# Forming the masked BK·AR products of both heads in one visit of TensorE, alternating row halves and PSUM banks, in a streaming encoder layer

## The chip, the cores and the metric

The kernel runs on one core of a Trainium2 chip. The metric is the device time of one execution in microseconds. The time before is the median of three runs.

## The reference

One layer of a hybrid encoder: differential attention and an RWKV-7 recurrence side by side, fed by one projection and closed by one output projection. Cut to what the change touches:

```
proj = rms_norm(x) @ w_in                        # 1024 prompt + 32 sample tokens, 2048 -> 8320 columns
q, k, v, g_att, p_rw, g_rw = split(proj)
att = diff_attention(q, k, v) * silu(g_att)      # 8 heads, two maps each
r, k, v, w, a = ...                              # token shift and LoRAs of p_rw; 16 heads of 64
for t in tokens:                                 # per head, S is 64 x 64
    sa = S @ a_t
    S = S * w_t + sa b_t^T + v_t k_t^T
    y_t = S @ r_t
out = x + concat(att, norm(y) * silu(g_rw)) @ w_out
```

The kernel works through the recurrence in chunks of 64 tokens. For each chunk and head it needs the products of the scaled keys with the scaled queries inside the chunk: `BK` (64 channels x two sets of 64 tokens) against `AR` (the same shape), 128 x 128 numbers, masked to the causal triangle.

## The kernel before, in words

**Tiling.** The tokens are worked in two halves: half A with 544 columns (512 prompt, 32 sample; 9 chunks) and half B with 512 (8 chunks). A unit `u` (0 to 15) is one half and one of 8 head pairs: one attention head and two RWKV heads, whose 64 channels lie in partitions 0 to 63 (`low`) and 64 to 127 (`high`). Per unit the main loop runs eight projections (`proj`, line 353), each a run of matmuls of 128 columns of weights against 256, 288 or 512 tokens into a PSUM tile `pj`; every weight is split into a rounded part and a remainder (`wh`, `wl`), every input likewise (`xh`, `xl`), so that three matmuls stand for one product. After the units come 16 output projections for each half.

**Who goes between.** Everything else is written as generators in six streams (`chs`, `dns`, `qks`, `pos`, `ats`, `los`). Between groups of projection matmuls `pump` (line 156) lets each stream take a step that is due. A step yields the nanoseconds after which the next may follow, and, if it names one, the PSUM bank that it wants. `clk` is the planner's own count of TensorE time, to which `mm` (line 83) adds what it takes a matmul to cost; `ready` says when it takes a bank to be free (900 ns after use for `am`, 2208 for `Y`, from the table `LAT`). This fixes the order of the program when it is built; on the chip the engines keep that order and wait on semaphores. PSUM has one buffer of `am` (attention, the block sums `blkr` of q and k, the post-processing) and one of `Y` (all that `rw_down` and `rw_decay` form).

**The step of the change.** `rw_down` (line 718) prepares a sub-block of a head pair: four or five chunks. The chunks are taken four at a time, so a sub-block of five has a second group of one chunk. For each group and each of the two heads there is one visit: wait for `Y`, form `BK` times `AR` for each chunk into its 128 columns of the bank (line 762, booked under line 92), and let VectorE multiply by the mask into `MM` (line 765). The matmuls are full fp32, which shows as two records each in the trace; they use 64 rows of the array, the lower ones for head 0, the upper for head 1. Behind them `MM` goes out by DMA, a forward substitution on VectorE (lines 784 and 786) solves it, and `rw_chain` goes on.

Of the kernel before, what the change touches and what calls it, by code (L numbers as in the profile page):

```python
# [12 lines left out]
F32R = mybir.dt.float32r  # L13
# [33 lines left out]
def build(tc, I, O):  # L47
# [16 lines left out]
    clk = [0.0]  # L64
    ready = {"am": 0.0, "Y": 0.0}

    def am():
        ready["am"] = None
        return PT("am", 1)

    def ym():
        ready["Y"] = None
        return PT("Y", 1)
# [6 lines left out]
            clk[0] += 95.0  # L80
            mode[0] = now

    def mm(out, lhsT, rhs, start=True, stop=True):
        n, m = 1, 1
        for d in rhs.shape[1:]:
            n *= d
        for d in lhsT.shape[1:]:
            m *= d
        shaped(lhsT.shape[0], m)
        load = 0.83 * m + 5.0  # L90
        clk[0] += max(0.4375 * n + 6.0, load) if rhs.dtype == F32R else 2 * max(0.84 * n, load)
        PE.matmul(out, lhsT, rhs, start=start, stop=stop)  # L92

    def tr(out, in_, idn):
# [9 lines left out]
    class Stream:  # L104
# [11 lines left out]
        def due(self):  # L116
            if self.cur is None and not self.q or self.cond is not None and not self.cond():
                return None
            return max(self.at, ready[self.am]) if self.am else self.at

        def run(self):
            c = clk[0]
# [3 lines left out]
        def step(self):  # L126
            if self.cur is None:
                if not self.q:
                    return False
                self.cur = self.q.pop(0)  # L130
            if self.cond is not None and not self.cond():
                return False
            if self.due() > clk[0]:
                return False
            self.cond, self.am = None, None
            try:
                y = next(self.cur[1])
            except StopIteration:
                self.done.add(self.cur[0])
                self.cur = None  # L140
                y = 0
            for r in ready:
                if ready[r] is None:
                    ready[r] = clk[0] + LAT[r]
            if callable(y):
                self.cond = y
            elif isinstance(y, tuple):
                self.at, self.am = clk[0] + y[0], y[1]
            else:
                self.at = clk[0] + y  # L150
            return True
# [106 lines left out]
    for k, tag in enumerate(RAW):  # L258
# [7 lines left out]
        a, eng = (acc[1], G) if pool else (acc[0], V)  # L266
# [131 lines left out]
    low, high = slice(0, 64), slice(64, 128)  # L398
# [9 lines left out]
    def lat(key, half):  # L408
        return LAT[key + "AB"[half]]
# [308 lines left out]
    def rw_down(half, i, sub, st):  # L718
# [8 lines left out]
        c_, a = st["ca"][:, 0, lo:hi], st["ca"][:, 1, lo:hi]  # L727
        P3 = st["P3"][:, lo:hi]
        r, k, v = st["rk"][:, 0, lo:hi], st["rk"][:, 1, lo:hi], st["v"][:, lo:hi]
        BK = T([128, cn, 2, 64], "BK")  # L730
# [22 lines left out]
        key = "ms"  # L753
        for c0 in range(0, cn, 4):
            m = min(4, cn - c0)
            for h in range(2):
                yield lat(key, half), "Y"
                key = "ms2"
                hr = (low, high)[h]
                p = ym()  # L760
                for j in range(m):
                    mm(p[:, 128 * j:128 * j + 128],
                       BK[hr, c0 + j].rearrange("p a t -> p (a t)"),
                       AR[hr, c0 + j].rearrange("p a t -> p (a t)"))
                V.tensor_tensor(MM[:, c0:c0 + m, h, :].rearrange("p c (x t) -> p c x t", t=64)[:, :, 0:3:2, :],  # L765
                                p[:, :128 * m].rearrange("p (a x t) -> p a x t", x=2, t=64),
                                mask.rearrange("p (x t) -> p x t", x=2).unsqueeze(1).to_broadcast([128, m, 2, 64]),
                                op=ALU.mult)
        MMg = MM.rearrange("p c h t -> p (c h) t")
# [390 lines left out]
```

## Time and the profile before

| | |
|---|---|
| time, median of 3 runs | 2612.89 us (2607.87 to 2619.28) |
| the profiled execution | 2613.46 us; span 2611.7 us from its first to its last instruction |
| TensorE matmul busy | 2549.7 us, 98% |
| TensorE weight load busy | 2220.1 us, 85% |
| VectorE busy | 1892.0 us, 72% |
| ScalarE, GpSimd busy | 1349.6 us (52%), 415.1 us (16%) |
| granted TensorE clock, mean | 0.995 of full speed |

Busy times are shares of the whole span. A matmul's record is longer than the time that it takes from its neighbours, since records overlap; what one costs is read from the starts.

### The profile page before, as it was taken

To read this page: it belongs to the slowest core of one execution; us is meant where nothing else is said; L and a number is where in the kernel's file an instruction comes from. 1 tells how busy PE (TensorE), PEld (TensorE's weight loads), DVE (VectorE), ACT (ScalarE), POOL (GpSimd) and SP (SyncE) were. 2 spreads that over 40 slices of the span, in tenths; PEclk is the share of its full clock that TensorE was granted. 3 is DMA by queue.
4 is the path that set the end of the run, shared out by engine and by line. 5 is a ranking of instruction groups with operands and counts; after the bars stand their busy time and mean duration, and the time that the engine had idled before them with its cause. 6 is when DMAs were issued, how large, how long until landed. Compare 5 with 4: busy or idle time off the path is not lost. (4 is left out here: it accounts for less than half of the span.)

```text
span 2611.7 us, 49090 instructions
## 1 busy us (share of the span) xinstructions
PE 2549.7 (98%) x17128; PEld 2220.1 (85%) x17128; DVE 1892.0 (72%) x5768; ACT 1349.6 (52%) x3138; POOL 415.1 (16%) x949
## 2 busy tenths in 40 slices
PE   7999999999999999999999999999999999999999
PEld 7999999999898999877777777777777778999887
DVE  7576877777777787788787887788878888753432
ACT  6455555555555655565555555555555556332321
POOL 3211111111111111111111111111111111111000
PEclk9999999999999999999999999999999999999999
DMA  4433332324242524353332323232324244544443
GB/s 156 119 102 94 93 103 84 110 82 115 75 122 80 170 72 122 98 153 100 98 98 87 103 83 106 85 111 81 114 81 115 77 132 118 176 148 140 137 142 108
DMA packets 198665, 286.74 MB, mean 110 GB/s; under 512 B 102097, under 2 KB 115921, under 8 KB 198417
## 3 DMA queue, kind: packets, MB, share of 16 engines
q0 software_dynamic: 51088, 169.12, 21.8%
q1 hardware_dynamic: 147328, 114.47, 15.5%
q8 instruction: 136, 2.23, 0.4%
q14 instruction: 113, 0.92, 0.1%
HBM read 228.11 MB, written 37.51 MB: 102 GB/s over the span
## 5 line engine op out<-in xcount | busy, mean ns | idle before, releaser
L92 PE MATMUL pj<-xh,wh 128*128 128x256 f32 (+2 forms) x3888 | 1294.2, 333 | 7.7 <-ACT xh L248 6.7
L92 PE MATMUL pj<-xl,wh 128*128 128x256 f32 (+2 forms) x3888 | 1274.7, 328 | 5.0 <-DVE xl L249 5.0
L92 PE MATMUL pj<-xh,wl 128*128 128x256 f32 (+2 forms) x3888 | 1272.5, 327 | 1.1 <-DVE wl L225 1.1
L92 PEld LDWEIGHTS pj<-xh,wh 128*128 128x128 f32 x3888 | 735.7, 189 | 61.2 <-ACT xh L248 7.0
L92 PEld LDWEIGHTS pj<-xl,wh 128*128 128x128 f32 x3888 | 736.2, 189 | 52.5 <-DVE xl L249 8.8
L92 PEld LDWEIGHTS pj<-xh,wl 128*128 128x128 f32 x3888 | 735.4, 189 | 52.4 <-DVE wl L225 2.1
L224 ACT CAST wh<-wr 128x512 fp32r<-128x512 f32 x584 | 360.6, 618 | 471.8 <-PE pj L92 420.1
L225 DVE TENSOR_TENSOR wl<-wr,wh 128x512 fp32r<-128x512 f32 x584 | 401.2, 688 | 193.5 <-ACT wh L224 162.9
L231 POOL DMA_DIRECT2D wr<-w_in x517 | 278.3, 538 | 1639.8 <-DVE wl L225 492.2
L786 DVE TENSOR_TENSOR ts<-tm,ts 64x54 f32<-64x54 f32 (+35 forms) x992 | 198.2, 200 | 15.1
L784 DVE TENSOR_TENSOR tm<-ts,ms 64x54 f32<-64x54 f32 (+35 forms) x992 | 197.7, 199 | 14.5 <-DMA ts<-tinit 0.2
L92 PEld LDWEIGHTS ch<-UV,MM 64*64 64x64 f32 (+2 forms) x1632 | 111.5, 145 | 38.1 <-DVE UV L903 9.2
L92 PE MATMUL ch<-UV,MM 64*64 64x64 f32 (+2 forms) x1632 | 128.9, 231 | 8.0 <-DVE UV L846 5.1
L899 ACT ACTIVATE SP<-Sw,PL 64x64 f32<-64x64 f32 x256 | 88.3, 345 | 91.2 <-DVE Sw L908 78.1
L225 DVE TENSOR_TENSOR wl<-MM,wh 128x512 fp32r<-128x512 f32 x64 | 44.0, 689 | 89.1 <-ACT wh L224 89.1
L224 ACT CAST wh<-MM 128x512 fp32r<-128x512 f32 x64 | 39.6, 620 | 128.9 <-PE pj L92 123.3
L896 DVE TENSOR_TENSOR xs<-ch,MM 64x64 f32<-64x64 f32 x272 | 58.6, 216 | 50.2 <-ACT RS L893 45.7
L908 DVE SCALAR_TENSOR_TENSOR Sw<-ch,PL,SP 64x64 f32<-64x64 f32 x256 | 70.7, 276 | 23.2 <-PE ch L92 16.7
L92 PE MATMUL am<-Vt,E 128*128 128x128 f32 (+1 forms) x592 | 84.7, 280 | 1.8 <-ACT wh L224 1.1
L92 PE MATMUL Y<-AR,BK 64*128 64x128 f32 x544 | 84.8, 290 | 0.7 <-DVE MM L765 0.6
L92 PEld LDWEIGHTS Y<-AR,BK 64*128 64x128 f32 x544 | 67.5, 188 | 19.8 <-issue 9.1
L92 PEld LDWEIGHTS am<-Vt,E 128*128 128x128 f32 (+1 forms) x592 | 73.5, 189 | 8.7 <-issue 2.6
(303 smaller groups left out, 3127.9 us busy)
## 6 DMA issues: line engine op xcount, KB each, us to landing
wr<-w_in POOLq DMA_DIRECT2D x517, 256.0 KB, 3.2
wr<-w_out POOLq DMA_DIRECT2D x64, 256.0 KB, 3.6
MM<-w_out POOLq DMA_DIRECT2D x32, 512.0 KB, 4.0
t<-xB SPq DMA_DIRECT2D x32, 256.0 KB
ms<-dm SPq DMA_DIRECT2D x96, 64.0 KB
t<-t SPq DMA_DIRECT2D x64, 68.0 KB
t<-mixd SPq DMA_DIRECT2D x16, 272.0 KB
t<-xA SPq DMA_DIRECT2D x16, 272.0 KB
```

Of the source, the lines that this page charges most:

```text
L92: PE.matmul(out, lhsT, rhs, start=start, stop=stop)
L224: S.copy(wh, raw)
L225: V.tensor_tensor(wl, raw, wh.bitcast(F32), op=ALU.subtract)
L231: q.dma_start(raw, wsrc[:, g * 512:(g + 1) * 512].rearrange("p (k f) -> p k f", k=4))
L784: V.tensor_tensor(tm, ts_[:, 0:qn, s:s + 1].to_broadcast([R * nb, qn, m]), ms[:, s:s + 1, s + 1:32].to_broadcast([R * nb, qn, m]), op=ALU. ...
L786: V.tensor_tensor(ts_[:, 0:qn, s + 1:32], tm, ts_[:, 0:qn, s + 1:32], op=ALU.add)
L896: V.tensor_tensor(xs[64 * h:64 * h + 64], ch[low, 64 * h:64 * h + 64], MM[low, c, h, 0:64], op=ALU.add)
L899: S.activation(SP[:, h, :], S_[hr, h, :], AF.Copy, scale=PL[hr, 0, gc:gc + 1])
L908: V.scalar_tensor_tensor(S_[hr, h, :], ch[low, 192 + 64 * h:256 + 64 * h], PL[low, h, gc:gc + 1], SP[:, h, :], ALU.mult, ALU.add)
```

## The change

The two visits of the two heads become one. It asks for both banks, `Y` for head 0 and `am` for head 1, and issues the chunks' matmuls in turn, low rows into `Y`, high rows into `am`. The two VectorE multiplications follow. The planner learns three things: a matmul may be booked at half its cost (`ways=2`), a step may name several banks, and it is due when the last of them is ready. The number of matmuls (272, 544 records), of VectorE multiplications (80) and of DMAs is as before.

```diff
-    def mm(out, lhsT, rhs, start=True, stop=True):
+    def mm(out, lhsT, rhs, start=True, stop=True, ways=1):
...
-        clk[0] += max(0.4375 * n + 6.0, load) if rhs.dtype == F32R else 2 * max(0.84 * n, load)
+        clk[0] += (max(0.4375 * n + 6.0, load) if rhs.dtype == F32R else 2 * max(0.84 * n, load)) / ways
...
-            return max(self.at, ready[self.am]) if self.am else self.at
+            return max(self.at, *(ready[a] for a in self.am)) if self.am else self.at
...
-                self.at, self.am = clk[0] + y[0], y[1]
+                self.at, self.am = clk[0] + y[0], y[1:]
...
         for c0 in range(0, cn, 4):
             m = min(4, cn - c0)
+            yield lat(key, half), "Y", "am"
+            key = "ms2"
+            ps2 = (ym(), am())
+            for j in range(m):
+                for h, hr in enumerate((low, high)):
+                    mm(ps2[h][:, 128 * j:128 * j + 128],
+                       BK[hr, c0 + j].rearrange("p a t -> p (a t)"),
+                       AR[hr, c0 + j].rearrange("p a t -> p (a t)"), ways=2)
             for h in range(2):
-                yield lat(key, half), "Y"
-                key = "ms2"
-                hr = (low, high)[h]
-                p = ym()
-                for j in range(m):
-                    mm(p[:, 128 * j:128 * j + 128],
-                       BK[hr, c0 + j].rearrange("p a t -> p (a t)"),
-                       AR[hr, c0 + j].rearrange("p a t -> p (a t)"))
                 V.tensor_tensor(MM[:, c0:c0 + m, h, :].rearrange("p c (x t) -> p c x t", t=64)[:, :, 0:3:2, :],
-                                p[:, :128 * m].rearrange("p (a x t) -> p a x t", x=2, t=64),
+                                ps2[h][:, :128 * m].rearrange("p (a x t) -> p a x t", x=2, t=64),
```

Since `clk` moves less, the whole order behind the first such visit is another one. Three places show it.

On TensorE, the first visit of the program, as a difference (`Y_` and `am_` are the two PSUM banks, `sc_` the attention's transposes):

```order
-L92 MATMUL Y_1720<-AR_1615,BK_1551 128x128 x4
-L97 MATMUL sc_1727<-cst_250,E_294_1627 128x128 x4
+L92 MATMUL Y_1720<-AR_1615,BK_1551 128x128
+L92 MATMUL am_1721<-AR_1615,BK_1551 128x128
+L92 MATMUL Y_1720<-AR_1615,BK_1551 128x128
+L92 MATMUL am_1721<-AR_1615,BK_1551 128x128
+L92 MATMUL Y_1720<-AR_1615,BK_1551 128x128
+L92 MATMUL am_1721<-AR_1615,BK_1551 128x128
+L92 MATMUL Y_1720<-AR_1615,BK_1551 128x128
+L92 MATMUL am_1721<-AR_1615,BK_1551 128x128
+L97 MATMUL sc_1841<-cst_250,E_294_1627 128x128 x4
```

Four matmuls of one head became eight that alternate; the second visit, which stood 27 rows further on, is gone.

On TensorE again, the visit of unit 10's second sub-block (half B), which runs among the projections of unit 11. Before, where the block sum of q, `am_22528<-p,blkr`, stands three and two rows above the first that is shown:

```order
L92 MATMUL pj_22497<-xl_2894_15717,wh_22518 128x512
L92 MATMUL pj_22497<-xh_2893_15716,wl_22519 128x512
L92 MATMUL pj_22497<-xh_2896_15722,wh_22518 128x512
L92 MATMUL pj_22497<-xl_2897_15723,wh_22518 128x512
L92 MATMUL pj_22497<-xh_2896_15722,wl_22519 128x512
L92 MATMUL pj_22497<-xh_2917_15828,wh_22552 128x512
L92 MATMUL pj_22497<-xl_2918_15829,wh_22552 128x512
L92 MATMUL pj_22497<-xh_2917_15828,wl_22553 128x512
L92 MATMUL pj_22497<-xh_2920_15834,wh_22552 128x512
L92 MATMUL pj_22497<-xl_2921_15835,wh_22552 128x512
L92 MATMUL pj_22497<-xh_2920_15834,wl_22553 128x512
L92 MATMUL Y_22562<-AR_22464,BK_22419 128x128 x4
```

And of the change, from the last matmul of the visit on:

```order
L92 MATMUL am_22529<-AR_22446,BK_22403 128x128
L92 MATMUL pj_22497<-xh_2897_15729,wh_22518 128x512
L92 MATMUL pj_22497<-xl_2898_15730,wh_22518 128x512
L92 MATMUL pj_22497<-xh_2897_15729,wl_22519 128x512
L92 MATMUL pj_22497<-xh_2900_15735,wh_22518 128x512
L92 MATMUL pj_22497<-xl_2901_15736,wh_22518 128x512
L92 MATMUL pj_22497<-xh_2900_15735,wl_22519 128x512
L92 MATMUL pj_22497<-xh_2948_15932,wh_22672 128x512
L92 MATMUL am_22654<-p_4398_22487,blkr_252 128x512
L92 MATMUL am_22654<-p_4399_22488,blkr_252 128x512
```

The visit now stands ahead of the block sum, and seven projection matmuls lie between the last use of `am` and the next. The same seven stand there for units 8, 10, 12 and 14. In half A there are seven places with 12 or 13 projection matmuls of 256 to 288 tokens between a visit and a block sum in `am`: five behind the one-chunk group and two (units 1 and 4) behind the group of four.

On VectorE at the same place, the change's rows up to the second mask multiplication:

```order
L786 TENSOR_TENSOR ts_22157<-tm_22186,ts_22157 64x3x22
L784 TENSOR_TENSOR tm_22189<-ts_22157,ms_22152 64x63
L786 TENSOR_TENSOR ts_22157<-tm_22189,ts_22157 64x3x21
L225 TENSOR_TENSOR wl_22704<-wr_22701,wh_22703 128x512
L784 TENSOR_TENSOR tm_22192<-ts_22157,ms_22152 64x60
L402 TENSOR_TENSOR p_4399_22488<-t_22484,p_4398_22487 128x512
L786 TENSOR_TENSOR ts_22157<-tm_22192,ts_22157 64x3x20
L402 TENSOR_TENSOR kk_22692<-bo_22689,p_4450_22691 128x256
L784 TENSOR_TENSOR tm_22195<-ts_22157,ms_22152 64x76
L765 TENSOR_TENSOR MM_22454<-Y_22528,cst_250 128x4x2x64
L786 TENSOR_TENSOR ts_22157<-tm_22195,ts_22157 64x4x19
L765 TENSOR_TENSOR MM_22454<-am_22529,cst_250 128x4x2x64
```

The write of `BK` by line 750, for which the visit waits, stands six rows above the first one shown (between them lie rows of lines 784, 351, 786, 803 and 784). The multiplication that empties `am` is the 17th row behind it.

## Rows read from the trace of the kernel before

**Rows 1.** The page's parts 1 and 2: busy time, share of the span and instructions of each engine; the granted clock in 40 slices, in tenths.

```profile
span 2611.7 us, 49090 instructions
PE 2549.7 (98%) x17128; PEld 2220.1 (85%) x17128; DVE 1892.0 (72%) x5768; ACT 1349.6 (52%) x3138; POOL 415.1 (16%) x949
PEclk9999999999999999999999999999999999999999
```

**Rows 2.** The end of the chain that ended last, in order of time: start, us, what.

```profile
2342.09 265.94 PE pj L92 x1476
2608.05 0.69 DVE t L968
```

**Rows 3.** The groups of the step, shapes kept apart: line, engine, operation, count | busy us, mean ns | idle before.

```profile
L92 PE MATMUL Y<-AR,BK 64*128 64x128 f32 x544 | 84.8, 290 | 0.7 <-DVE MM L765 0.6
L765 DVE TENSOR_TENSOR MM<-Y,cst 128x512 f32<-128x512 f32 x64 | 43.7, 682 | 4.4 <-PE Y L92 3.9
L765 DVE TENSOR_TENSOR MM<-Y,cst 128x128 f32<-128x128 f32 x16 | 4.6, 285 | 1.5 <-PE Y L92 1.1
```

**Rows 4.** The timeline around a visit of four chunks (eight records), TensorE and then the VectorE row that empties the bank: start us, us, engine, line, tiles.

```profile
146.68 0.29 PE L92 MATMUL pj<-xl,wh 128*128 128x288 f32 x1
146.81 0.29 PE L92 MATMUL pj<-xh,wl 128*128 128x288 f32 x1
147.04 1.16 PE L92 MATMUL Y<-AR,BK 64*128 64x128 f32 x8
148.12 0.40 PE L92 MATMUL pj<-xh,wh 128*128 128x288 f32 x1
...
148.24 0.68 DVE L765 TENSOR_TENSOR MM<-Y,cst 128x512 f32<-128x512 f32 x1
```

**Rows 5.** The same around a visit of one chunk (two records), and the VectorE row that empties the bank.

```profile
179.76 0.29 PE L92 MATMUL pj<-xh,wl 128*128 128x288 f32 x1
179.99 0.48 PE L92 MATMUL Y<-AR,BK 64*128 64x128 f32 x2
180.40 0.40 PE L92 MATMUL pj<-xh,wh 128*128 128x288 f32 x1
...
182.51 0.28 DVE L765 TENSOR_TENSOR MM<-Y,cst 128x128 f32<-128x128 f32 x1
```

**Rows 6.** The timeline of TensorE around two visits of line 863: matmuls of 64 rows and 64 columns whose outputs alternate between partitions 0 to 63 and 64 to 127; 16 records, and 20.

```profile
210.67 0.29 PE L92 MATMUL pj<-xl,wh 128*128 128x288 f32 x1
210.90 0.68 PE L92 MATMUL ch<-UV,MM 64*64 64x64 f32 x16
211.51 0.40 PE L92 MATMUL pj<-xh,wl 128*128 128x288 f32 x1
...
255.86 0.29 PE L92 MATMUL pj<-xh,wl 128*128 128x288 f32 x1
256.09 0.80 PE L92 MATMUL ch<-UV,MM 64*64 64x64 f32 x20
256.81 0.40 PE L92 MATMUL pj<-xh,wh 128*128 128x288 f32 x1
```

**Rows 7.** The timeline of TensorE at line 906: weights of 128 columns, 64 moving columns, four records.

```profile
223.47 0.63 PE L92 MATMUL ch<-UV,MM 128*128 128x64 f32 x4
223.91 0.36 PE L92 MATMUL pj<-xh,wl 128*128 128x256 f32 x1
```

**Rows 8.** The timeline at a visit of four chunks in half A (second sub-block), TensorE and the VectorE row that empties its bank.

```profile
310.26 1.16 PE L92 MATMUL Y<-AR,BK 64*128 64x128 f32 x8
...
312.33 0.68 DVE L765 TENSOR_TENSOR MM<-Y,cst 128x512 f32<-128x512 f32 x1
```

**Rows 9.** The timeline at the two visits of unit 10's second sub-block (half B), TensorE and VectorE in order of time. In brackets is the idle time before a row, and what ended it.

```profile
1569.02 0.41 DVE L750 TENSOR_TENSOR BK<-rk,ca 128x256 f32<-128x256 f32 x1
1569.35 0.22 DVE L786 TENSOR_TENSOR ts<-tm,ts 64x72 f32<-64x72 f32 x1
1569.50 0.34 DVE L514 SCALAR_TENSOR_TENSOR asg<-am,cvec,asg 128x128 f32<-128x128 f32 x1
1569.90 0.68 DVE L402 TENSOR_TENSOR p<-t,p 128x512 fp32r<-128x512 f32 x1
...
1569.98 0.47 PE L92 MATMUL am<-p,blkr 128*128 128x512 f32 x1 [0.91 <-DVE tm L784]
1571.22 0.39 PE L92 MATMUL pj<-xh,wh 128*128 128x512 f32 x1
1571.45 0.39 PE L92 MATMUL pj<-xl,wh 128*128 128x512 f32 x1
...
1571.46 0.47 DVE L803 SCALAR_TENSOR_TENSOR bo<-rk,par 128x256 f32<-128x256 f32 x1
1572.00 1.16 PE L92 MATMUL Y<-AR,BK 64*128 64x128 f32 x8
1578.25 0.68 DVE L765 TENSOR_TENSOR MM<-Y,cst 128x512 f32<-128x512 f32 x1
1579.07 1.13 PE L92 MATMUL Y<-AR,BK 64*128 64x128 f32 x8 [0.40 <-DVE MM L765]
```

**Rows 10.** Groups of VectorE that stand in the queue there: line, operation, count | busy us, mean ns of one | idle before.

```profile
L225 DVE TENSOR_TENSOR wl<-wr,wh 128x512 fp32r<-128x512 f32 x584 | 401.2, 688 | 193.5 <-ACT wh L224 162.9 <-PE pj L92 20.4 <-PE Y L92 3.2
L351 DVE TENSOR_TENSOR t<-pj,rb 128x512 f32<-128x512 f32 x24 | 16.3, 680 | 0.8 <-PE pj L92 0.6
L402 DVE TENSOR_TENSOR kk<-bo,p 128x256 fp32r<-128x256 f32 x24 | 10.0, 416 | 0.5 <-ACT p L401 0.5
L786 DVE TENSOR_TENSOR ts<-tm,ts 64x60 f32<-64x60 f32 x72 | 15.0, 209 | 1.2
```

## The prediction

> **What bounds the kernel now.** I read the page first. TensorE is busy for 98% of the span at a full granted clock; no other engine passes 72%, weight loads apart [rows 1]. The chain that ended last closes with 266 us of projection matmuls without a wait and one VectorE addition [rows 2]. So a microsecond less on TensorE is a microsecond less in the end, as long as no new wait takes its place, and one less on VectorE is worth nothing by itself. Next I read the groups of the step: 544 records of `Y<-AR,BK`, and 64 + 16 mask multiplications, which tells that there are 64 visits of four chunks and 16 of one [rows 3]. What a visit costs is in the timeline, from the starts of its neighbours: two projection matmuls start 0.13 us apart; with a visit of eight records between them it is 1.31 us (146.81 to 148.12), so the visit takes 1.18 [rows 4]. The visit of two records takes 0.64 - 0.13 = 0.51 [rows 5]. Six records more cost 0.67, so a record costs 0.112, and 0.51 - 2 x 0.112 = 0.29 us is a fixed price for going to 64 rows and coming back. In all the step holds TensorE for 64 x 1.18 + 16 x 0.51 = 83.7 us.
>
> **What goes, part one: the fixed price.** Eighty visits become forty: 32 of sixteen records and 8 of four. That saves 40 x 0.29 = 11.6 us however the records run, since alternation stays within one shape (64 rows, 128 columns).
>
> **Part two: whether the two row halves overlap.** The trace of before has no visit that alternates rows. Its nearest rows alternate columns, at line 863. Sixteen records take 0.84 - 0.13 = 0.71 us there, twenty take 0.82 [rows 6]: 0.11 for four more, 0.029 each (the starts carry two decimals). Alone, a record of 64 columns should take half of what 128 take, 0.056. So alternation between two parts of the array runs nearly two at a time, weight loads included, at 0.52 of the price. By that a record of the new visit costs 0.0585, a visit of sixteen 0.29 + 16 x 0.0585 = 1.23 in place of 2.36, one of four 0.52 in place of 1.02. The sum is 32 x 1.13 + 8 x 0.50 = 40.2 us, fixed price included. The other end is no overlap at all: records go on at 0.112 and 11.6 us stay. What speaks for that end is line 906: weights of 128 columns against only 64 moving columns take 0.44 us for four records [rows 7], again 0.11, so loading 128 columns is by itself as dear as a record, and if two row halves share one way for their weights nothing can overlap. The column rows show two loads of 64 columns side by side, not two of 128. I take 40.2, as that row is the only one in which two parts of the array alternate.
>
> The Trainium skill, "TensorE: Matmul & The Clock Gate", section "Part 3: Packing small matmuls — row/col tiling", has matmuls of separate row tiles run concurrently and gives 3.07x for four of them, not the full four. As an estimate from that page, two tiles at the same efficiency would be 1.53x, a record 0.073, the saving 32 us. No run here shows it yet, and the sum does not use it.
>
> **Part three: what is added, the wait for `am`.** VectorE does the same 80 multiplications. But head 1's product now sits in `am`, which the block sums and the attention want back, and VectorE empties it second. What counts is how late VectorE comes and how soon TensorE wants the bank.
> - Behind a visit of one chunk VectorE came 2.04 us after the last record's end (180.47 to 182.51) in one place [rows 5] and 0.04 us after a visit of four in another (148.20 to 148.24) [rows 4]. In the changed order five one-chunk visits are followed by a block sum after 12 or 13 projection matmuls, which is 1.5 us behind that end. Two multiplications of 0.285 [rows 3] after 2.04 free the bank at 2.6: a stall of 1.1. After 0.04 there is none. I take half, 5 x 0.55 = 2.8 (0 to 5.6).
> - At two places in half A a group of four is followed as soon. VectorE came 0.91 late in such a place (311.42 to 312.33) [rows 8]; with 2 x 0.68 the bank is free at 2.27, 0.8 after it is wanted: 1.6 in all (0 to 1.6).
> - At four places of half B the visit moves ahead of a block sum that used to precede it. Behind the write of `BK` VectorE has 17 rows up to the second multiplication: ten of 0.21, and 0.68, 0.47, 0.69, 0.68, 0.42 and twice 0.68 [rows 3, 9, 10], 6.4 us by durations and some 5.1 with the 0.075 by which neighbours overlap (1569.43 against 1569.35) [rows 9]. TensorE wants `am` after the visit (1.23) and seven matmuls at 0.23 [rows 9], 2.9 us after `BK`: a stall of 2.2. Before, TensorE idled there for 0.91, waiting for `am`, and for 0.40 at the second visit [rows 9]. The first wait stays, as the visit needs `am` and `BK` as well; the second goes. Net 4 x 1.8 = 7.2. If TensorE comes as late as it did (1572.00, 2.6 behind `BK`) nothing stalls and 4 x 1.3 = 5.2 is won; without overlap on VectorE it is 4 x (3.5 - 0.4) = 12.4.
>
> Together 11.6 us, from -5.2 to 19.6. Behind a stalled block sum stand the projection matmuls themselves, so nothing hides it; ScalarE's square roots and the rotary step follow later and are not on the path.
>
> **Priced at nothing.** A second wait of one visit per group falls away, so the forward substitution starts a few microseconds sooner; it is VectorE work under TensorE, and VectorE has 28% to spare [rows 1]. The two multiplications come back to back, which holds a weight split (0.69, line 225) up by at most 0.68 per visit; without its cover by the weights already split that would be 40 x 0.68 = 27 us, but the idle time before matmuls of `Y<-AR,BK` that a late multiplication caused was 0.6 us in the whole span [rows 3]. The rest of the order is the same work at other places.
>
> **The sum.** The profiled execution took 2613.46 us (span 2611.7 and 1.8 around it), 0.6 over the median of 2612.89. 2613.5 - 40.2 + 11.6 = 2584.9, so **2585 us**, 1.1% less.
>
> **The rivals.** A measurement of this kernel can tell about 0.5%, 13 us, from no change.
> - *No overlap.* Loading 128 columns of weights is the limit in both row halves. Then 2613.5 - 11.6 + 11.6 = 2613: the change doesn't do what it says. For it: the 0.11 of line 906 [rows 7]. Against it: the column rows [rows 6], whose loads ran side by side. 13%.
> - *Half an overlap.* A record costs 0.085, midway: a visit of sixteen 1.65, of four 0.63, saving 32 x 0.71 + 8 x 0.39 = 25.8; 2613.5 - 25.8 + 11.6 = 2599 us. It needs a part of each record, its load or its start, that stays serial; the 0.029 for 0.028 of the column rows speaks against one [rows 6]. 12%. (The Trainium skill's 3.07x, cited above, points this way.)
> - *VectorE empties `am` too late (slower).* In 20 or so places the bank is wanted within some 2 us. If VectorE lagged there as it did behind the visit at 1572.00, 5.1 us (1573.16 to 1578.25) [rows 9], each would stall for 5.1 + 1.36 - 1.5 = 5.0: 2613.5 - 40.2 + 20 x 5.0 = 2673. It loses from 40.2 / 20 = 2.0 us a place, by more than 0.5% from 2.7. Against it: in that stretch VectorE had rows ahead that the changed order puts elsewhere, and in half A the lags are 0.04 to 2.04. 7%. The Trainium skill, "TensorEngine Tiling (Array Packing)", section "PSUM Bottleneck", warns of just this: tiling speeds TensorE up and not the emptying of PSUM. The trace agrees in that line 765's time can't shrink [rows 3].
> - *The forecast*, overlap with the waits of part three, 2568 to 2597: 68%.
>
> **Range and chances.** The low end is the overlap with the least waits, 2613.5 - 40.2 - 5.2 = 2568; the high end is no overlap, 2613. Beyond it lie the late `am` and little else. The likeliest case's own range is 2568 to 2597. Faster by over 0.5% (under 2600): 68% and two thirds of the half overlap, 76%. Within: no overlap and the rest of the half, 17%. Slower: 7%.
>
> **What would show it.** In the profile after, the records of a visit of sixteen should span about as long as eight do now, 1.2 us, with starts in pairs; if they span 2.0 there is no overlap and the forecast is wrong by 29 us. TensorE's busy time should fall with the span. Idle time ahead of the block sums `am<-p,blkr` that ends with line 765 prices part three; over 1 us a visit would break the forecast, and a stall at a place of which nothing is said here would, too.

## The result, and the profile after

The changed kernel takes 2600.78 us (median of 20 executions, 2594.68 to 2609.74) against 2614.46 us for the kernel before in the same session: a ratio of 0.9945, 95% interval 0.9933 to 0.9956. That is 14 us less, a little under half of the 28.6 forecast; the median lies inside the range, and the forecast of 2585 was 16 us too low. One execution of the experiment e12 took 5011 us, nearly twice as long as its others, and is left out of every figure below.

The page's heads, answering to [rows 1], and the mean granted clock:

```profile
span 2603.7 us, 49027 instructions
PE 2518.3 (97%) x17128; PEld 2205.2 (85%) x17128; DVE 1897.8 (73%) x5768; ACT 1347.3 (52%) x3138; POOL 418.6 (16%) x949
PEclk9999999999999899999999999999999999999999
```

```profile
core 0: 2603.7 us, clock 0.986
```

TensorE is busy 31 us less, but the span fell by only 8, and one slice of the clock shows an 8 where [rows 1] had none. The mean clock was 0.995 before. The profiled execution took 2605.68 us and is one of the slower of the 20.

**The step itself** came out as forecast. The groups, answering to [rows 3], and the first visit, answering to [rows 4] (start us, us, engine, line, tiles):

```profile
L92 PE MATMUL Y<-AR,BK 64*128 64x128 f32 x272 | 41.6, 288 | 0.0
L92 PE MATMUL am<-AR,BK 64*128 64x128 f32 x272 | 41.4, 288 | 0.4 <-DVE asg L514 0.4
L765 DVE TENSOR_TENSOR MM<-Y,cst 128x512 f32<-128x512 f32 x32 | 21.9, 683 | 0.4
L765 DVE TENSOR_TENSOR MM<-am,cst 128x512 f32<-128x512 f32 x32 | 21.8, 680 | 1.1 <-PE am L92 1.1
```

```profile
140.75 0.28 PE L92 MATMUL pj<-xh,wl 128*128 128x256 f32 x1
140.96 0.37 PE L92 MATMUL Y<-AR,BK 64*128 64x128 f32 x1
140.96 0.37 PE L92 MATMUL am<-AR,BK 64*128 64x128 f32 x1
141.17 0.27 PE L92 MATMUL Y<-AR,BK 64*128 64x128 f32 x1
141.18 0.27 PE L92 MATMUL am<-AR,BK 64*128 64x128 f32 x1
141.28 0.27 PE L92 MATMUL Y<-AR,BK 64*128 64x128 f32 x1
141.29 0.27 PE L92 MATMUL am<-AR,BK 64*128 64x128 f32 x1
...
141.85 0.27 PE L92 MATMUL am<-AR,BK 64*128 64x128 f32 x1
142.05 0.66 PE L97 MATMUL sc<-cst,E 128*128 128x128 f32 x4
```

The records start in pairs 0.007 us apart, and a pair follows a pair after 0.11: two at a time, 0.056 a record against 0.112. The sixteen take 1.09 us from the first start to the next instruction, where eight took 1.08. Summed over all visits from the starts of neighbouring records, with the entry into 64 rows counted alike in both traces, the step's price fell from 88.4 to 50.5 us: 37.9 of the 40.2 forecast. Both ends lie above the forecast's 83.7 and 43.5. The new visits cost 7.0 us more, because TensorE's order as built does not alternate everywhere: at 1124, 1824 and 2087 us, for instance, the eight records of one head stand ahead of the eight of the other. The old ones cost 4.7 more, because some of the 80 visits are broken in two (90 groups of records).

**Where the rest went** is in TensorE's waits. From the list of waits, the longest in sum first (engine, line, what it waited for: us in total, times, longest), of before and then of after:

```profile
PE ch L92 <- DVE xs L896: 7.0, 16, 1.6
...
PE ch L92 <- DVE Yt L916: 6.1, 12, 0.8
PE ch L92 <- DVE UV L846: 5.1, 7, 1.2
```

```profile
...
PE ch L92 <- DVE UV L846: 8.5, 10, 2.2
...
PE ch L92 <- ACT UV L851: 5.2, 4, 1.7
...
PE pj L92 <- DVE t L351: 4.0, 4, 1.6
...
PE Y L97 <- DVE MM L765: 2.6, 2, 1.4
...
PE am L97 <- DVE MM L765: 1.4, 3, 0.6
```

The rows of `ch` that wait for line 846 or 851 are the first two steps of a chain (lines 848 to 855). The first needs what comes back from the forward substitution by DMA, transposed on VectorE (line 846); the second needs ScalarE's copy of the first step's result (line 851). What held these two engines can be seen one step further back. ScalarE and VectorE in front of the first step at 1723 us, then ScalarE in front of the second step at 2120 us:

```profile
1721.64 0.62 ACT L224 CAST wh<-wr 128x512 fp32r<-128x512 f32 x1 [2.57 <-DMA wr<-w_in]
1722.29 0.69 DVE L225 TENSOR_TENSOR wl<-wr,wh 128x512 fp32r<-128x512 f32 x1 [3.03 <-ACT wh L224]
1722.90 0.42 DVE L846 STREAM_TRANSPOSE UV<-k 32x256 f32<-32x256 f32 x1
...
2119.44 0.62 ACT L224 CAST wh<-wr 128x512 fp32r<-128x512 f32 x1 [2.72 <-DMA wr<-w_in]
2120.08 0.36 ACT L851 COPY UV<-ch 32x256 f32<-32x256 f32 x1
```

The transposition and the copy stand in their engine's order behind the split of a weight (lines 224 and 225), and the split waited for the DMA of that weight. The same holds at 478, 1199, 1593, 1857 and 1986 us, where ScalarE waited 1.7 to 2.7 us for a weight. Whether the transposition's own data had landed by then is not in the record; at 1723 its DMA had been issued 7.1 us before.

I summed all gaps of over 0.6 us between the starts of neighbouring TensorE records, less 0.23 each, from 30 us to 3 us before the end: 36.2 us before (48 gaps), 62.6 after (72). Ahead of a chain's first two steps they grew from 6.2 to 15.9 (10.4 of it in the seven places just named), ahead of projections from 1.8 to 8.3, ahead of work that wants `am` or `Y` back from line 765 from 0.6 to some 10. The list names line 765 for a third of these last gaps only; each of them ends 0.06 to 0.15 us behind the row of line 765 that empties the bank.

The worst place is one that the prediction says nothing of. The timeline of TensorE at 892 us (in brackets the idle time ahead and what ended it), and the windows of the same 17 us in after and in before (us, busy us of PE, PEld, DVE, ACT and POOL with instructions, granted clock, DMA):

```profile
892.72 0.69 PE L92 MATMUL ch<-UV,MM 32*32 32x32 f32 x16
895.05 0.69 PE L92 MATMUL ch<-k,UV 32*32 32x32 f32 x16 [1.65 <-ACT UV L851]
896.78 1.12 PE L92 MATMUL ch<-UV,MM 64*64 64x64 f32 x16 [1.04 <-ACT TT L858]
898.79 0.77 PE L92 MATMUL ch<-Sw,AR 128*128 128x128 f32 x2 [0.89 <-ACT MM L865]
900.60 0.66 PE L92 MATMUL ch<-xs,TT 128*128 128x64 f32 x2 [1.04 <-ACT ca L704]
902.72 1.11 PE L92 MATMUL ch<-UV,MM 128*128 128x64 f32 x4 [1.46 <-DVE UV L903]
906.02 0.77 PE L92 MATMUL ch<-Sw,AR 128*128 128x128 f32 x2 [2.19 <-DVE Yt L916]
908.41 0.58 PE L92 MATMUL pj<-xh,wh 128*128 128x256 f32 x1 [1.62 <-DVE t L351]
```

```profile
896.00:913.00 17.00, 9.01 (x48) 7.95 (x49) 13.10 (x52) 6.02 (x15) 0.53 (x3) 0.50 0.26 80
```

```profile
896.00:913.00 17.00, 16.54 (x150) 15.72 (x149) 9.82 (x22) 6.75 (x15) 2.37 (x5) 1.00 0.59 167
```

Seven chain steps, each of which needs the one before by way of ScalarE or VectorE, stand back to back with no projection between them: 15.7 us for 58 records. And the granted clock is at its lower level (0.50, 1.2 GHz) for all of the 17 us from 896 on.

**The clock** is the second place. Between the start and the end, where both are alike, the trace of before has 13.7 us at the lower level in two stretches, that of after 64.9 us in ten. Seven of the ten begin within 4.3 us of the start of a wait of 0.9 to 2.4 us (from start to start) at a chain step, one (872 us) behind a wait of 1.5 us for `Y`, and two with no gap over 0.6 us in the 7 us ahead of them. One of them in the timeline, and then the windows of the 6.8 us behind it and behind the wait at 1986 us:

```profile
1720.84 0.38 PE L97 MATMUL am<-cst,t 128*128 128x128 f32 x2
1723.38 0.40 PE L92 MATMUL ch<-UV,MM 32*32 32x32 f32 x7 [2.15 <-DVE UV L846]
```

```profile
1725.20:1732.00 6.80, 6.80 (x39) 5.19 (x37) 2.89 (x11) 3.31 (x8) 0.54 (x1) 0.50 0.11 37
...
1988.00:1994.80 6.80, 6.80 (x44) 5.26 (x44) 2.20 (x7) 2.96 (x8) 0.54 (x1) 0.50 0.09 33
```

TensorE is busy for all of 6.80 us there and gets through little more than half the work; its projection matmuls start 0.43 us apart, where they start 0.23 apart at full clock [rows 9]:

```profile
1730.90 0.63 PE L92 MATMUL pj<-xh,wl 128*128 128x512 f32 x1
1731.33 0.63 PE L92 MATMUL pj<-xh,wh 128*128 128x512 f32 x1
```

Not every such wait is followed by this: 1.68 us at 1856 were not.

The account of the two profiled executions, in us: step -37.9; gaps over 0.6 us +26.4; records drawn out at the low clock (each start-to-start under 0.6 us less the median of the same pair at full clock: 28.1 after, 7.0 before) +21.1; all smaller delays, which are the remainder and not broken down, -17.6; together -8.0, 2611.7 to 2603.7. Over all executions there is a simpler one. Span times mean clock (what is left if every us at half clock counts half) is steady from execution to execution: 2567.3 us with a standard deviation of 1.5 for the changed kernel, whose times have one of 3.9. For before it is 2599.2 in the session of e1 to e4. So at full clock the change is worth 31.9 us, and 18.7 of them go back: the clock takes 31.3 us per execution after, 12.6 before (mean clock 0.9879 and 0.9952). In the other sessions of the experiments the kernel before has 2595.4 to 2599.4 for the product and 10.3 to 14.8 us for the clock, so the two numbers stand for 28 to 32 and 16 to 21 us. The 21.1 of the records belongs to the profiled pair, whose execution after had a lower clock (0.986) than the mean.

### The profile page after: what moved, and what is told of

It reads as the page before. It is cut to its first block, busy times and chain, and to the rows that moved or that the text cites. A ratio compares the mean times of both kernels' runs of the same rounds, so it can differ in the third digit from the quotient of the medians.

```text
span 2603.7 us, 49027 instructions
## 1 busy us (share of the span) xinstructions
PE 2518.3 (97%) x17128; PEld 2205.2 (85%) x17128; DVE 1897.8 (73%) x5768; ACT 1347.3 (52%) x3138; POOL 418.6 (16%) x949
## 3 DMA queue, kind: packets, MB, share of 16 engines
q0 software_dynamic: 51088, 169.12, 21.7%
## 4 chain that ended last, share of the span: by engine, by line
PE 66%; DVE 17%; ACT 6%; DMA 6%; issue 5%; SPq 0%; POOL 0%; DVEq 0%; ACTq 0%; POOLq 0%
PE pj L92 49%; PE ch L92 7%; DVE wl L225 3%; PE am L92 3%; PE sc L92 3%; DMA wr<-w_in 2%; DVE ts L786 2%; DVE tm L784 2%; ACT wh L224 2%; PE Y L92 2%; PE sc L97 1%; PE am L97 1%; DVE Sw L908 1%; DMA wr<-w_out 1%; DVE MM L765 1%
## 5 line engine op out<-in xcount | busy, mean ns | idle before, releaser
L92 PE MATMUL am<-Vt,E 128*128 128x128 f32 (+1 forms) x592 | 83.7, 278 | 0.6 <-ACT E L571 0.5
L558 ACT ACTIVATE E<-sc,sm 128x640 f32<-128x640 f32 (+3 forms) x64 | 61.1, 954 | 40.4 <-DVE sm L557 40.1
L92 PE MATMUL sc<-Ks,Qd 128*128 128x512 f32 (+2 forms) x224 | 74.9, 346 | 1.0 <-DMA Ks<-t 0.7
```

Of the source, the lines that this page charges most:

```text
L558: S.activation(E[c][:, :nk], sc[:, :nk], AF.Exp, bias=mx[:, c:c + 1], scale=SCALE, accum_out=l[:, c:c + 1])
```

## The experiments

Two questions: is the overlap worth what the starts say, and by which cause; and where does the other half of the gain stay. All kernels in one table. Waits are the gaps over 0.6 us of one profiled execution, in all and ahead of a chain's first two steps; clock and product are means over the executions; the first row is from the session of e1 to e4. The kernel before had medians from 2608.3 to 2614.5 us in the different sessions, so kernels of different sessions are compared by the ratio, which is to the kernel before of the same session. A profiled execution need not be typical: e5's, at 2600.2, is the slowest of its six, and e3's, at 2617.6, the second slowest of 12.

| kernel | median us | ratio to before (95%) | clock | span x clock | waits | chain start |
|---|---|---|---|---|---|---|
| before | 2612.9 | 1 | 0.9952 | 2599 | 36 | 6.2 |
| after | 2600.8 | 0.9945 (0.9933 to 0.9956) | 0.9879 | 2567 | 63 | 15.9 |
| e1, before, visit booked at half | 2603.6 | 0.9956 (0.9940 to 0.9972) | 0.9936 | 2585 | 37 | 8.8 |
| e8, before, `Y` 2400 | 2605.9 | 0.9984 (0.9973 to 0.9994) | 0.9943 | 2589 | 35 | 6.2 |
| e12, before, chain due 2 us later | 2605.2 | 0.9982 (0.9966 to 0.9997) | 0.9952 | 2591 | 28 | 8.2 |
| e2, head after head | 2593.6 | 0.9916 (0.9900 to 0.9932) | 0.9907 | 2567 | 47 | 11.0 |
| e3, booked at full price | 2610.1 | 0.9980 (0.9963 to 0.9998) | 0.9853 | 2569 | 61 | 16.6 |
| e6, both heads low rows | 2614.9 | 1.0017 (1.0002 to 1.0031) | 0.9863 | 2578 | 53 | 15.7 |
| e4, `am` later | 2586.8 | 0.9896 (0.9879 to 0.9913) | 0.9916 | 2565 | 45 | 17.2 |
| e5, `am` later, units 4 and 5 | 2590.4 | 0.9932 (0.9915 to 0.9949) | 0.9913 | 2568 | 52 | 15.3 |
| e7, `am` later, half A | 2601.7 | 0.9962 (0.9944 to 0.9979) | 0.9873 | 2567 | 50 | 21.7 |
| e9, filler in six waits | 2596.3 | 0.9957 (0.9945 to 0.9969) | 0.9914 | 2572 | 55 | 6.0 |
| e13, chain due 1 us later | 2580.5 | 0.9874 (0.9851 to 0.9896) | 0.9928 | 2561 | 57 | 7.3 |
| e10, chain due 2 us later | 2565.0 | 0.9836 (0.9823 to 0.9848) | 0.9952 | 2551 | 45 | 2.6 |
| e14, chain due 4 us later | 2576.8 | 0.9857 (0.9836 to 0.9879) | 0.9935 | 2558 | 54 | 8.3 |
| e15, the same 2 us, half B alone | 2588.2 | 0.9901 (0.9878 to 0.9925) | 0.9915 | 2565 | 54 | 6.0 |
| e11, e10 and e4 together | 2567.3 | 0.9848 (0.9832 to 0.9863) | 0.9948 | 2553 | 38 | 7.5 |

### The step: rows or banks, and what the overlap is worth

**e6.** Same order, row for row; the other row half gets no work.

```diff
-                       BK[hr, c0 + j].rearrange("p a t -> p (a t)"),
-                       AR[hr, c0 + j].rearrange("p a t -> p (a t)"), ways=2)
+                       BK[low, c0 + j].rearrange("p a t -> p (a t)"),
+                       AR[low, c0 + j].rearrange("p a t -> p (a t)"), ways=2)
```

> The changed kernel with the same order, row for row, but head 1's products formed from head 0's operands in rows 0 to 63 (head 1's share of the products is left out, so the work in the other row half is gone); the records still alternate between the two banks. Theory A (records run two at a time because they sit in different row halves): a record costs 0.112 us again, the step 544 x 0.112 + 48 x 0.29 = 75 us in place of 50.5, and the kernel takes about 24 us more, 2620 to 2630 us. Theory B (it is the second PSUM bank that lets the next record start): the starts stay in pairs and the time is that of the changed kernel, within 4 us.

The start of its first visit:

```profile
142.91 0.48 PE L92 MATMUL Y<-AR,BK 64*128 64x128 f32 x2
143.24 0.38 PE L92 MATMUL am<-AR,BK 64*128 64x128 f32 x2
143.46 0.38 PE L92 MATMUL Y<-AR,BK 64*128 64x128 f32 x2
143.69 0.38 PE L92 MATMUL am<-AR,BK 64*128 64x128 f32 x2
```

The banks still alternate and nothing overlaps: four records per 0.45 us, 0.112 each, and the step is back at 74.8 us (forecast 75). So the second bank alone does not make the overlap, and the other row half is needed. Two row halves that write one bank were not run. The time rose by 0.0072 of 2614, 19 us, where 24 were added: waits fell from 63 to 53. Some of the work that goes back in fills waits.

**e2.** The two inner loops exchanged, so that one head's records follow the other's.

```diff
-            for j in range(m):
-                for h, hr in enumerate((low, high)):
+            for h, hr in enumerate((low, high)):
+                for j in range(m):
```

> The changed kernel with its joint visit, both banks and its half price in the planner, but head 0's matmuls all first and then head 1's; the order outside the visits is nearly that of the change (277 rows differ). A record then costs 0.112 again. If the overlap reaches the end of the kernel in full: 25 to 29 us slower than the change, some 12 us slower than before. If TensorE would have waited at these places anyway: under 12 us slower than the change.

Both missed: it is faster than the changed kernel by 0.0029 (some 7 us). The edit did not do what I meant, since TensorE's order as built mixes the heads in the middle of a visit; by the starts three of eight pairs overlap and a visit takes 1.64 us in place of 1.09. The step costs 13 us more, the waits shrink by 16, span times clock is the same, and the difference is the clock's. Thirteen microseconds more of TensorE's own work cost nothing here, as they came in place of waits.

### Whether the order alone moves the time

**e1, e8** (before) and **e3** (changed) keep the work and move the planner's bookings only: old visits at half price; `Y` back after 2400 ns in place of 2208; the new visit at full price.

```diff
# e1, on the kernel before
-                       AR[hr, c0 + j].rearrange("p a t -> p (a t)"))
+                       AR[hr, c0 + j].rearrange("p a t -> p (a t)"), ways=2)
# e8, on the kernel before
-  Y=2208,
+  Y=2400,
# e3, on the changed kernel
-                       AR[hr, c0 + j].rearrange("p a t -> p (a t)"), ways=2)
+                       AR[hr, c0 + j].rearrange("p a t -> p (a t)"))
```

> The kernel before with its two visits per group, in turn and one bank each; only the planner books their matmuls at half their cost, as the change does. The chip does the same work, in another order (2334 of some 13400 TensorE rows differ). Theory A (the overlap is worth its 38 us and the shared bank am brings the new waits): the time of before within 5 us. Theory B (the order of before fits the chip and any other one costs, whatever its cause): 8 to 20 us slower than before.

> The kernel before with one number of the planner's table changed, Y from 2208 to 2400, which puts rows at other places of TensorE's order and leaves every instruction as it was. Theory A (the order alone is worth some 10 us either way): the time differs from that of the kernel before by 4 to 15 us, in either direction. Theory B (the same work at other places costs the same, as the prediction had it): within 3 us, 2609 to 2616 us.

> The changed kernel, joint and alternating, but booked in the planner at full price (ways=1), so that its clock runs slower than in the change. Theory A (shared bank): steps that follow a visit are planned no later, the waits stay, within 4 us of the change. Theory C (the planner's clock runs ahead of the chip, so that steps come too early and TensorE waits): 5 to 12 us faster than the change. Theory B: anything within 10 us either way.

e1 is 11 us faster than before by the ratio, outside both theories; e8 4 us faster (the lower end of theory A); e3 9 us slower than the changed kernel, at the lowest clock of all. So an order with the same instructions is worth up to some 10 us either way. That the planner's cheaper booking is what hurts finds no support: at full price the chain starts wait just as long (16.6), and at half price in the kernel before they wait 8.8.

### Which waits

**e4, e7, e5.** The planner is told that `am` is back 2.7 us after the visit: in all units, in half A, in units 4 and 5 of half A.

```diff
                        AR[hr, c0 + j].rearrange("p a t -> p (a t)"), ways=2)
+            ready["am"] = clk[0] + 2700          # e7: if half == 0; e5: if half == 0 and i in (4, 5)
```

> The change with one line more: behind a joint visit the planner takes am to be free after 2700 ns in place of 900, which is about when line 765 has emptied it in the profile of the change. Theory A: the eleven long gaps ahead of am users behind line 765 (10.2 us in the profile of the change, 7.6 above normal starts) go, and with them a part of the stretches at the low clock: 7 to 12 us faster than the change. Theory B: a new order with new waits, within 5 us of the change.

> The changed kernel, with the planner told at the visits of units 4 and 5 alone that `am` comes back 2.7 us after the visit. TensorE's order differs from the changed kernel's only before 910 us or so; the four decay passes of unit 6 come up to 18 projection matmuls sooner, and the seven chain steps that stood back to back at 892 us are spread between projections again. Theory A (about half of what was missing is this one pile-up, its wait of some 11 us and the low clock of 17 us behind it): 13 to 20 us less than the changed kernel, 2581 to 2588 us. Theory B (the missing microseconds are spread thinly over all the visits, and the pile-up only holds waiting that would fall elsewhere): within 5 us of the changed kernel, 2596 to 2602 us.

> The changed kernel, with the later `am` told to the planner in all units of half A and in none of half B. Theory A (the pile-up of unit 6 is what the later `am` cured): the time of the kernel that has it in units 4 and 5 alone, within 5 us, 2581 to 2590 us. Theory B (it is worth something at every visit): half of the 14 us that the later `am` gave in both halves, 2592 to 2596 us, and less than half of that for units 4 and 5 alone.

e4 gained 0.0049, 13 us, and I took the pile-up at 892 us, which its order does not have, for the reason. e5 and e7 let that fall. e5 removes the pile-up with little else (its order is the changed kernel's up to 701 us and again from some 965 on), its 17 us at the low clock are gone, and it is only 0.0013 faster, 3 us, less than the intervals tell apart. e7, with the later `am` in all of half A and no pile-up, is 0.0017 slower. In their traces the low stretches behind the chain starts of half B are still there (6.8 us each at 1716, 1979 and 2112 us in e5, at 1721, 1984 and 2117 in e7); in e4, which has e7's order throughout half A, one low stretch is left there (10.2 us at 2102). So what e4 gained came in half B. The low stretches are those of one execution each, and e5's was a slow one.

**e9.** Work for TensorE in six of these waits; its result is overwritten.

```diff
         p = PT("ch", 1)
+        if gsub in (22, 26, 30):                 # ahead of the second step: (20, 24, 28)
+            for _ in range(6):
+                PE.matmul(p[:, 0:512], blkr, XH[0][:, 0:512], start=True, stop=True)
```

> The changed kernel, with six matmuls of 128 rows and 512 columns put ahead of six chain steps of half B, into the same `ch` bank, whose result is overwritten: the steps that waited for 2.43, 1.95 and 1.48 us (chain starts of units 11, 13 and 15) and for 1.13, 1.68 and 2.16 us (second steps of units 10, 12 and 14). The filler is 36 x 0.227 = 8.2 us of TensorE work and the six waits hold 9.5 us beyond an ordinary step. Theory A (the low clock behind these steps comes of the wait itself): the low stretches at 1725, 1988 and 2121 us go, the mean granted clock rises from 0.988 to 0.991 or more, and the kernel with more work takes 5 to 10 us less than the changed kernel, 2590 to 2596 us. Theory B (the low clock falls where it falls, whatever TensorE does): the clock stays at 0.988 and the time at that of the changed kernel or up to 8 us more, 2600 to 2609 us.

The timeline where the changed kernel was idle for 2.15 us at 1723, and at a second step; then the windows behind the first, behind the next chain start of this kind, and behind that second step:

```profile
1715.42 1.55 PE L851 MATMUL ch<-xh,blkr 128*128 128x512 f32 x6
1716.81 0.39 PE L92 MATMUL pj<-xh,wh 128*128 128x512 f32 x1
...
2111.40 1.79 PE L859 MATMUL ch<-xh,blkr 128*128 128x512 f32 x6 [1.78 <-ACT UV L854]
```

```profile
1718.00:1726.00 8.00, 7.96 (x64) 6.18 (x63) 5.62 (x23) 5.10 (x11) 1.07 (x2) 1.00 0.31 97
...
1982.00:1990.00 8.00, 7.88 (x53) 6.14 (x51) 6.37 (x24) 5.60 (x11) 0.54 (x1) 1.00 0.20 66
2113.00:2123.00 10.00, 10.00 (x52) 7.69 (x52) 4.20 (x17) 2.81 (x8) 0.00 (x0) 0.50 0.10 26
```

At the three chain starts the wait is filled and the clock stays at 1.00 where it had fallen at 1725 and 1988. At the three second steps the filler had to wait itself, as it writes the bank that ScalarE (line 854 of this kernel) had not read out, and behind the 2.25 us between starts at 2111 the clock is low for 10 us. The mean clock rose from 0.9879 to 0.9914 and gave back 9 us, the filler and its waits cost 5, and against before the ratio is no better than the changed kernel's. The mechanism is shown at two places, the forecast of 5 to 10 us less was not met.

**e10, e13, e14, e15, e12.** The planner takes the forward substitution to end later; no instruction is added. A chain starts when `yield max(1500, t_m + lat("tt", half) - clk[0])` is due, and `t_m` counts from the planner's clock at the visit or, where that is later, from the planned end of the substitution before (line 791). The edits are to `ttA` and `ttB`: 2 us, 1 us, 4 us, 2 us in half B alone, and 2 us in the kernel before.

```diff
-ttA=13941, ttB=14740
+ttA=15941, ttB=16740                             # e10; e12 on the kernel before
# e13: 14941, 15740;  e14: 17941, 18740;  e15: ttB=16740 alone
```

> The changed kernel, with the planner told that the forward substitution ends 2 us later (ttA 13941 to 15941, ttB 14740 to 16740); no instruction is added or removed, the order differs in some 2100 rows. Theory A (the chain starts come too early for the shortened step, wait for the substitution, and each wait is followed by the low clock): waits ahead of the chain's first two steps fall from 15.9 to under 8 us, the mean granted clock rises to 0.991 or more, 2582 to 2592 us. Theory B (waiting is only moved): the sum of waits over 0.6 us stays at 55 to 70 us, and the time within 5 us of the changed kernel, 2596 to 2606 us.

> The kernel before, with the same 2 us on the forward substitution (ttA and ttB). Theory A (the waits at the chain starts are the change's own): there are 6 us of them in all here, so at most 4 to 6 us less than the kernel before. Theory B (the planner's table is loose in both kernels): 10 us or more less, and what the cured changed kernel gains over the kernel before is not the change's alone.

> The changed kernel with the forward substitution taken to end 1 us later (ttA, ttB plus 1000). Theory A (the chain came due too early, by 1 to 2 us): the gain lies between, waits ahead of the chain's first two steps at 5 to 10 us, 2572 to 2590 us. Theory B (the kernel with 2 us later met a lucky order): no relation, the time as likely above 2590 us as below, and the waits ahead of the chain's start don't go with the time.

> The changed kernel with the forward substitution taken to end 4 us later. Theory A: the waits ahead of the chain's first two steps stay under 4 us, and the time at that of 2 us later, within 10 us: 2560 to 2575 us, or a little more as the chains now end later. Theory B: a third order, 2580 us or more.

> The changed kernel with the forward substitution taken to end 2 us later in half B alone; half A, with the pile-up at 892 us, keeps its order row for row. Theory A: the waits of half B ahead of the chain's first two steps (some 11 us) and the low stretches behind them (24 us) go, 15 to 20 us less than the changed kernel, 2581 to 2587 us. Theory B (most of what 2 us later gained was the pile-up and other places of half A): under 10 us less, 2591 to 2601 us.

The first line of e10's page, its clock and one of its waits:

```profile
span 2564.5 us, 48999 instructions
```

```profile
core 0: 2564.5 us, clock 0.996
```

```profile
PE ch L92 <- DVE UV L846: 2.8, 5, 1.6
```

e10 takes 2564.96 us, 1.6% less than before and, by the ratios, 28 us less than the changed kernel, more than theory A asked; the same two numbers give the kernel before 0.2% (e12), as its theory A had it. Its step costs what the changed kernel's does (51.9 us by the starts), its waits are 18 us fewer, and the clock takes 12 us in place of 31. In half B alone (e15), with half A and its pile-up left row for row, the gain over the changed kernel is 0.0044, 11.5 us, between theory A's 15 to 20 and theory B's 10; the intervals reach into both. With 1 us it is 18.6 (chain starts at 7.3 us: both of theory A's numbers), with 4 us 23. The three shifts in both halves each have a lower ratio than every kernel of the table that leaves `tt` alone, though the intervals of e13 and e4 overlap. That the due time is a cause is shown. What it changes is when TensorE comes: ScalarE waits as long for weights in e10 (26.3 us at line 224 for `w_in`) as in the changed kernel (25.4), but two of the chain's first steps wait over 0.6 us behind such a weight, where seven did. That it explains the whole is not: e14's chain starts wait 8.3 us, more than e10's, where I expected under 4, and e13 and e14 still have the pile-up (17.1 us at the low clock at 889 and 883 us) which e10's order happens to lack. Some 5 to 10 of e10's 28 us over the changed kernel may be its order's luck, by the distance to its neighbours on both sides; which of its waits make them stays open.

**e11.** Both corrections.

```diff
-ttA=13941, ttB=14740
+ttA=15941, ttB=16740
                        AR[hr, c0 + j].rearrange("p a t -> p (a t)"), ways=2)
+            ready["am"] = clk[0] + 2700
```

> The changed kernel with both of the planner's numbers corrected: `am` back 2.7 us after the visit in all units, and the forward substitution 2 us later. Theory A: the two cures add, span times clock near 2560 us and a clock of 0.994, 2573 to 2583 us. Theory B: the order's luck decides, 2585 to 2600 us.

2567.3 us, better than theory A asked, but no better than e10: the two do not add. With the chain due later, a later `am` has nothing left to win.

## Why the prediction was half right

- **Fixed price and overlap, 40.2 us: right.** 37.9 by the starts; two at a time to within 1%, and not without the second row half (e6). The forecast's 0.52 rests on half of 0.112 as the price of a lone 64-column record, which no run shows; the visits of before and after give the ratio directly. The doubt that line 906 raised [rows 7] did not hold: two loads of 128 columns in different row halves do go side by side. That the sum misses by only 2 us is in part luck: the new visits cost 7.0 us more than forecast, where the built order undoes the alternation, and the old ones 4.7. Both could have been read from the built order.
- **The waits for `am`, 11.6 us: near in sum, not place by place.** Eleven gaps that line 765's release of `am` ended are together 7.6 us longer than ordinary, two at `Y<-cst,BK` 2.7. Half A had 5.1 of the 7.6 where 4.4 were forecast, half B 2.6 where 7.2 were (net of the second visits' waits that fall away), and the waits for `Y` were not forecast. That the sum comes near is in part luck. The rival of a far too late `am` (5 us in 20 places) did not come.
- **The step that failed is "priced at nothing".** It holds two sentences. The first: the forward substitution starts a few microseconds sooner, it is VectorE work under TensorE. It does: counted from the last write of `BK` ahead of the visits, its first row comes after 29.3 us where it took 34.8 in half A, and after 28.4 for 31.0 in half B (means over 16 each). The visits end sooner by more, 7.4 and 4.4 us, so it now starts some 2 us later behind them. What was priced at nothing is the other side: the planner counts the chain's due time from the visit as well, and TensorE waited 9.7 us more ahead of the chain's first two steps, mostly where VectorE or ScalarE was held by a weight that had not landed. I looked at whom the sooner substitution would hold up, and not at what else is timed by the visit. That the due time is a cause is shown (e10, e13, e14); why it fits worse than before stays open, since the substitution's last multiplication comes as late behind the visits as it did (53.5 us for 53.7 in half A, 53.3 for 53.2 in half B). The second: the rest of the order is the same work at other places. That is not free either: the seven gaps at 892 us alone are 10.7 of the 62.6 us, and e1, e3 and e8 show that an order alone is worth up to 10 us either way. The range had no term for that.
- **The clock was taken as given.** [Rows 1] shows it full, and so every wait was priced at its own length. After the change the waits are fewer than 3% of the span, but stretches at the lower level follow some of them and take some 20 us more than before (21.1 by the records of the profiled pair, 16 to 21 by span times clock). By span times clock that is the whole gap between forecast and result: -31.9 at full clock, where -28.6 was forecast, and +18.7. That the part at full clock came near is luck again. The profiled pair fell short of the forecast by 20.6 us, and these are 2.3 of the step, 14.8 of waits beyond the 11.6 that were priced, 21.1 of the clock, and -17.6 of smaller delays, which were not forecast. The Trainium skill, "TensorE: Matmul & The Clock Gate", section "HAM oscillation — how this bites in real kernels", tells of the like in a kernel that waits for DMA: the array is throttled behind a wait and the work after it starts cold. The windows at 1725 and 1988 us agree (0.50 for 6.8 us, TensorE busy throughout), and e9's filled waits too.

## What to carry to other kernels

Where an engine's order is fixed by a table of measured delays, a shorter step can leave the delays that are counted from it too short: look for what is timed by the step, and try later times for it (here two numbers were worth more than the change had brought by itself). Where a wait ends with another engine, look at what that engine had waited for: here it was a weight's DMA, two steps back. Price a wait on TensorE with the low clock that may follow it, and compare kernels by span times granted clock beside their times: it separates the work and the waits from the clock, and within a session it is steadier. A forecast for a kernel with a planned order needs a term of its own for the order, here some 10 us in 2600.

## What the runs showed that was not expected

- Executions of one and the same kernel differ by the clock: the changed kernel took from 2594.7 us at a mean clock of 0.991 to 2609.7 at 0.984, 2.4 us for 0.001, while span times clock stayed at 2567.3.
- More work on TensorE can make the kernel faster, or cost less than itself: e2's step is 13 us dearer and the kernel 7 us faster; e6 adds 24 us and loses 19.
- Whether the low clock follows a wait is not told by its length alone: behind 1.95 us (1986) it did, behind 1.68 us (1856) not, behind a row of waits of 1.2 to 2.6 us (895 to 908, from start to start like the others) it stayed low for 17.1 us.
